# Row sums of a 16384 x 1024 array: each 16-row load made by two transfers, of even and of odd partitions

## The chip, the cores and the metric

The kernel runs on one core of a Trainium2 chip. The metric is the device time of one execution in microseconds (us), taken as the median of several runs. Of the core's engines this kernel uses VectorE (DVE in the profile) and ScalarE (ACT) for the sums, and the queues of SyncE (SP) and ScalarE for issuing transfers between the device's main memory (DRAM) and the on-chip memory of 128 partitions. A transfer's packets are moved by the core's sixteen DMA engines.

## The reference

```python
def setup_inputs():
    batch, seq, dim = 32, 512, 1024
    return {"x": np.random.randn(batch, seq, dim).astype(np.float32)}

def reference(x):
    return np.sum(x, axis=-1).astype(np.float32)
```

So 32 x 512 = 16,384 rows of 1,024 float32 numbers are summed, each to one number: 67.1 MB are read and 65.5 KB written.

## The kernel before

The rows are spread over the 128 partitions, 128 rows to each. They come in two blocks (`BLOCKS = (112, 16)`): in the first, partition p holds rows 112p to 112p + 111 of the array; in the second, 16 consecutive rows of what is left. Inside a partition a block's rows lie one behind another in DRAM, so a transfer of 16 rows takes one contiguous run of 65,536 bytes for each partition.

**The full loads.** The loop `while c < whole` goes over the first block in steps of `G = 16` rows, seven steps. Each step takes one of three buffers `xt` (128 partitions of 16 x 1024 numbers) and fills it by SyncE's queue (line 89): 8,388,608 bytes, all 128 partitions in one transfer. The first step is split: one row of each partition first (512 KB), then the other 15. `rows_dve` (line 47) then lets VectorE sum the 16 rows of all partitions in one TENSOR_REDUCE, into columns of the tile `res`. Only in the seventh step does ScalarE take part: `rows_act` (line 55) sums 7 of the 16 rows, one ACTIVATE each with its sum in an accumulator, which a second instruction reads out. A load into a buffer waits until the reduce that used it three steps earlier has ended, so SyncE's queue stands at such a wait for most of the time, with the two following loads already issued.

**The first block's results.** When the seventh step's sums are done, `res` of the first block (128 x 112 numbers) is stored by two transfers on ScalarE's queue (line 99), one of partitions 0 to 103 and one of 104 to 127. In that queue they stand behind the seven ACTIVATEs and ahead of ScalarE's work on the last 16 rows.

**The tail.** The second block's 16 rows come in five smaller transfers on SyncE's queue: 9, 4 and 2 rows (line 105), and the last row in two pieces of 544 and 480 numbers into a tile of its own, `tail` (line 108). VectorE and ScalarE share the 9 and the 4 rows; of the next two, VectorE sums one by `pairs_dve` (line 67, adding the two halves of a row to each other and summing the pairs), ScalarE the other; VectorE sums the last row in two parts by the same function. At the end a no-op on SyncE's queue waits for ScalarE's last result, and the store of the second block's sums (line 128) waits for VectorE's last.

**What the kernel does to its own program.** After it is built, the first two load instructions of SyncE (`EARLY = 2`) are moved to the program's entry, ahead of the barrier there, so that they start at once; only a load that waits for nothing may be moved. Each transfer signals its end on one of eight semaphores, which are given out in turn; for every load each of the sixteen DMA engines adds one when its share has landed.

Of the kernel before, what the change touches and what calls it, by code (L numbers as in the profile page):

```python
# [1 line left out]

# [4 lines left out]

F32 = mybir.dt.float32
ADD = mybir.AluOpType.add
COPY = mybir.ActivationFunctionType.Copy  # L10
X = mybir.AxisListType.X

BLOCKS = (112, 16)
G = 16
ACT_ROWS = 7
CUT = 544
EARLY = 2


@with_exitstack  # L20
def row_sums(
    ctx: ExitStack,
    tc: tile.TileContext,
    x: bass.AP,
    out: bass.AP,
):
    nc = tc.nc
    P = nc.NUM_PARTITIONS

    x_flat = x.flatten_outer_dims()  # L30
    R, D = x_flat.shape
    C = R // P
    assert R % P == 0 and sum(BLOCKS) == C
    out_flat = out.rearrange("a (b c) -> (a b c)", c=1)

    xpool = ctx.enter_context(tc.tile_pool(name="x", bufs=3))
    rpool = ctx.enter_context(tc.tile_pool(name="res", bufs=1))


    tail = rpool.tile([P, D + 16], F32, name="tail")  # L40
    part = tail[:, CUT + 14 : CUT + 15]
    nc.vector.memset(tail[:, CUT + 15 : CUT + 16], 0.0)  # L42
    seen = rpool.tile([P, 2], F32, name="seen")
    pairs = [rpool.tile([P, D // 2], F32, name=f"pairs{i}") for i in range(3)]

    def rows_dve(xt, res, j, n, c):
        nc.vector.tensor_reduce(  # L47
            out=res[:, c : c + n],
            in_=xt[:, j * D : (j + n) * D].rearrange("p (j d) -> p j d", d=D),
            axis=X,  # L50
            op=ADD,
        )

    def sum_act(v, acc):
        return nc.scalar.activation(out=v, in_=v, func=COPY, accum_out=acc)  # L55

    by_act = []

    def rows_act(xt, res, j, n, c):
        for i in range(n):  # L60
            by_act.append(
                sum_act(xt[:, (j + i) * D : (j + i + 1) * D], res[:, c + i : c + i + 1])
            )

    def pairs_dve(v, a, b, acc, pairs):
        h = (a + b) // 2
        nc.vector.tensor_tensor_reduce(  # L67
            out=pairs[:, 0 : h - a], in0=v[:, a:h], in1=v[:, h:b], scale=1.0, scalar=0.0,
            op0=ADD, op1=ADD, accum_out=acc,
        )  # L70

    def block(r0, n):
        x_b = x_flat[r0 : r0 + P * n].rearrange("(p c) d -> p (c d)", p=P)
        out_b = out_flat[r0 : r0 + P * n].rearrange("(p c) -> p c", p=P)
        return x_b, out_b, rpool.tile([P, n], F32, name=f"res{r0}")

    full = C - G
    done = 0
    for b, n in enumerate(BLOCKS):
        x_b, out_b, res = block(done * P, n)  # L80
        final = b == len(BLOCKS) - 1
        whole = n - G if final else n
        c = 0
        while c < whole:
            m = min(G, whole - c)
            xt = xpool.tile([P, G * D], F32, tag="xt", name="xt")
            parts = (0, 1, m) if done + c == 0 else (0, m)
            for i, k in zip(parts, parts[1:]):
                nc.sync.dma_start(
                    out=xt[:, i * D : k * D], in_=x_b[:, (c + i) * D : (c + k) * D]  # L90
                )
            a = ACT_ROWS if done + c + m == full else 0
            rows_dve(xt, res, 0, m - a, c)
            rows_act(xt, res, m - a, a, c + m - a)
            c += m
        if not final:

            for i, k in ((0, 104), (104, P)):
                nc.scalar.dma_start(out=out_b[i:k], in_=res[i:k])
        done += n  # L100

    xt = xpool.tile([P, G * D], F32, tag="xt", name="xt")
    cuts = [0, 9, 13, 15]
    for i, k in zip(cuts, cuts[1:]):
        nc.sync.dma_start(out=xt[:, i * D : k * D], in_=x_b[:, (c + i) * D : (c + k) * D])  # L105
    last = 15 * D
    for i, k, gap in ((0, CUT, 0), (CUT, D, 16)):
        nc.sync.dma_start(
            out=tail[:, i + gap : k + gap],
            in_=x_b[:, c * D + last + i : c * D + last + k],  # L110
        )

    by_act.clear()
    for i, k in zip(cuts[:2], cuts[1:3]):
        h = (k - i) // 2
        rows_dve(xt, res, i, h, c + i)
        rows_act(xt, res, i + h, k - i - h, c + i + h)
    pairs_dve(xt, 13 * D, 14 * D, res[:, c + 13 : c + 14], pairs[2])
    rows_act(xt, res, 14, 1, c + 14)
    pairs_dve(tail, 0, CUT, part, pairs[0])  # L120


    nc.vector.tensor_copy(out=seen, in_=tail[:, CUT + 14 : CUT + 16])  # L123
    pairs_dve(tail, CUT + 14, D + 16, res[:, c + 15 : c + 16], pairs[1])


    tc.keep_in_program_order(nc.sync.keepalive_nop([nc.sync.lower_ap(res[:, c + 14 : c + 15])]))
    store = nc.sync.dma_start(out=out_b, in_=res)
    for i in by_act:
        tc.declare_no_dep(store.ins, i.ins, reason="the wait is in the nop before it")  # L130


def kernel(tc: tile.TileContext, x: bass.AP, out: bass.AP):
    row_sums(tc, x, out)
    tc.close()
    tc.compile()  # L136

    sp = mybir.EngineType.SP  # L140
    fn = tc.nc.m.functions[0]
    entry, body = None, None
    for blk in fn.blocks:
        ops = [i for i in blk.instructions if i.engine == sp]
        if entry is None:
            entry = blk
        elif any(i.opcode == "DMACopy" for i in ops):
            body = blk
            break
    code = list(body.instructions)  # L150
    loads = [i for i in code if i.engine == sp][:EARLY]
    for load in loads:
        assert load.opcode == "DMACopy" and not load.sync_info.on_wait
        code.remove(load)
    body.instructions = code
    code = list(entry.instructions)
    at = next(k for k, i in enumerate(code) if i.engine == sp and i.opcode == "Drain")
    code[at:at] = loads
    entry.instructions = code

# [1 line left out]
_INS = ['x']  # L162
_OUTS = [((32, 512), 'float32')]


# [23 lines left out]
```

## Time and profile before

| | us |
|---|---|
| median of 7 runs | 161.93 |
| lowest and highest | 161.81, 162.51 |
| the profiled execution | 162.51 |
| its span, first to last instruction | 160.7 |

In the span, by the page:

| engine | busy us | share |
|---|---|---|
| VectorE | 121.5 | 76% |
| ScalarE | 17.2 | 11% |
| GpSimd | 0.2 | 0% |

All x transfers run in one queue of SyncE, the first block's store in ScalarE's. Over the span 418 GB/s are moved on average.

How to read it: the span is cut into 40 slices of 4.02 us, and a row of digits or of GB/s has one entry for each. A packet counts whole in the slice in which it starts, and the large packets here take 2.4 us, so neighbouring slices swing between 294 and 522 GB/s though the transfers go on evenly; the mean over three of them is what counts. A timeline line gives the start, the duration, the engine (with a "q" for its queue), the line in the code, the operation, what it writes and reads, and in brackets the idle time before it and what ended that. A line of transfer issues gives minimum, median and maximum of the issue's own time in ns; the time from issue to landing stands apart. Lines of waits give the total, the number and the longest.

### The profile page before, as it was taken

How to read it: one execution, taken by the hardware profiler on the slowest of the kernel's cores; microseconds unless marked ns; L12 is line 12 of the kernel's file. 1: busy time of each engine (PE TensorE's matmuls, PEld its weight loads, DVE VectorE, ACT ScalarE, POOL GpSimd, SP SyncE). 2: the span in 40 equal slices, each digit the busy share in tenths (PEclk: the TensorE clock that was granted, in tenths of full speed). 3: DMA queues.
4: the chain of work that ended last, by engine and by line, in shares of the span. 5: the costliest groups of instructions: out<-in, count | busy, mean ns of one | idle time of the engine just before them, and what ended most of it. 6: DMA issues, size and time to landing. Idle time of an engine off the chain costs nothing.

```text
span 160.7 us, 122 instructions
## 1 busy us (share of the span) xinstructions
DVE 121.5 (76%) x17; ACT 17.2 (11%) x31; POOL 0.2 (0%) x4
## 2 busy tenths in 40 slices
DVE  0000049998699968999499994999949998598874
ACT  0000000000000000000000000000000000595892
POOL 0000000000000000000000000000000000000000
DMA  9996997997997996996996996996996996999990
GB/s 375 459 474 291 489 506 343 457 506 310 489 489 326 489 489 294 522 489 294 522 489 294 522 489 294 522 489 294 522 489 294 522 489 294 440 431 397 423 387 27
DMA packets 2170, 67.18 MB, mean 418 GB/s; under 512 B 506, under 2 KB 634, under 8 KB 890
## 3 DMA queue, kind: packets, MB, share of 16 engines
q1 hardware_dynamic: 2016, 67.12, 97.1%
q10 hardware_dynamic: 153, 0.06, 0.1%
q14 instruction: 1, 0.00, 0.0%
HBM read 67.11 MB, written 0.07 MB: 418 GB/s over the span
## 4 chain that ended last, share of the span: by engine, by line
DMA 75%; DVE 22%; SPq 0%; issue 0%; DVEq 0%
DMA xt<-in_x_dram 75%; DVE res L47 21%; DVE pairs L67 1%; SPq L105 0%; DVE seen L123 0%; DVE tail L67 0%; DVE res L67 0%; DVEq L136 0%
## 5 line engine op out<-in xcount | busy, mean ns | idle before, releaser
L47 DVE TENSOR_REDUCE res<-xt 128x16 f32<-128x16384 f32 (+3 forms) x9 | 119.8, 13309 | 35.2 <-DMA xt<-in_x_dram 35.2
L55 ACT ACT_TABLE_LOAD x1 | 1.3, 1283 | 138.3 <-DMA xt<-in_x_dram 138.3
L55 ACT ACTIVATE xt<-xt 128x1024 f32<-128x1024 f32 x15 | 15.6, 1044 | 2.4 <-DMA xt<-in_x_dram 2.4
L55 ACT ACTIVATION_READ_ACCUMULATOR xt<-xt 128x1 f32 x15 | 2.8, 187 | 0.0
L42 DVE MEMSET tail<- 128x1 f32 x1 | 0.1, 59 | 1.3 <-PEq L173 1.3
L67 DVE CUSTOM_DVE_ANT_0 pairs<-xt 128x512 f32<-128x512 f32 x1 | 0.7, 692 | 0.4 <-DMA xt<-in_x_dram 0.4
L67 DVE CUSTOM_DVE_ANT_0 pairs<-tail 128x272 f32<-128x272 f32 (+1 forms) x2 | 0.9, 428 | 0.0
L123 DVE COPY seen<-tail 128x2 f32<-128x2 f32 x1 | 0.2, 169 | 0.0
L67 DVE DVE_READ_ACCUMULATOR2_ANT res<- 128x1 f32 x2 | 0.2, 83 | 0.0
L173 POOL MEMSET const-uint8-127<- 128x1 uint8 x1 | 0.1, 102 | 0.0
L173 POOL MEMSET const-bfloat16-1.0<- 128x1 bf16 x1 | 0.1, 101 | 0.0
L173 POOL MEMSET const-float32-0.0<- 128x1 f32 x1 | 0.1, 98 | 0.2 <-issue 0.2
L173 POOL MEMSET const-float32-1.0<- 128x1 f32 x1 | 0.1, 98 | 0.0
L67 DVE DVE_READ_ACCUMULATOR2_ANT tail<- 128x1 f32 x1 | 0.1, 84 | 0.0
## 6 DMA issues: line engine op xcount, KB each, us to landing
xt<-in_x_dram SPq DMA_DIRECT2D x1, 7680.0 KB
xt<-in_x_dram SPq DMA_DIRECT2D x1, 4608.0 KB, 32.4
xt<-in_x_dram SPq DMA_DIRECT2D x1, 2048.0 KB, 36.9
xt<-in_x_dram SPq DMA_DIRECT2D x1, 1024.0 KB, 39.1
xt<-in_x_dram SPq DMA_DIRECT2D x1, 512.0 KB, 4.0
tail<-in_x_dram SPq DMA_DIRECT2D x1, 272.0 KB, 39.2
tail<-in_x_dram SPq DMA_DIRECT2D x1, 240.0 KB, 39.1
xt<-in_x_dram SPq DMA_DIRECT2D x6, 40.8
```

Source lines behind the costliest of these rows:

```text
L42: nc.vector.memset(tail[:, CUT + 15 : CUT + 16], 0.0)
L47: nc.vector.tensor_reduce(out=res[:, c : c + n], in_=xt[:, j * D : (j + n) * D].rearrange("p (j d) -> p j d", d=D), axis=X, op=ADD,)
L55: return nc.scalar.activation(out=v, in_=v, func=COPY, accum_out=acc)
L67: nc.vector.tensor_tensor_reduce(out=pairs[:, 0 : h - a], in0=v[:, a:h], in1=v[:, h:b], scale=1.0, scalar=0.0, op0=ADD, op1=ADD, accum_out ...
L123: nc.vector.tensor_copy(out=seen, in_=tail[:, CUT + 14 : CUT + 16])
L173: nc = _bacc.Bacc("TRN2", target_bir_lowering=False, num_devices=1)
```

## The change

Each of the seven full loads becomes two transfers on SyncE's queue, one of the 64 even partitions and one of the 64 odd ones (`q:P:2`), each of 64 runs of 65,536 bytes. The first step has the same two; its load of one row is gone, so that the two loads moved to the entry are the two halves of the first buffer. The first block's store is written in the program behind the tail's loads instead of ahead of them, and as four transfers, of partitions 0 to 103, 104 to 111, 112 to 119 and 120 to 127, on ScalarE's queue as before.

```diff
@@ -84,19 +84,18 @@
             xt = xpool.tile([P, G * D], F32, tag="xt", name="xt")
-            parts = (0, 1, m) if done + c == 0 else (0, m)
-            for i, k in zip(parts, parts[1:]):
+
+
+            for q in range(2):
                 nc.sync.dma_start(
-                    out=xt[:, i * D : k * D], in_=x_b[:, (c + i) * D : (c + k) * D]
+                    out=xt[q:P:2, 0 : m * D], in_=x_b[q:P:2, c * D : (c + m) * D]
                 )
             a = ACT_ROWS if done + c + m == full else 0
             rows_dve(xt, res, 0, m - a, c)
             rows_act(xt, res, m - a, a, c + m - a)
             c += m
         if not final:
-
-            for i, k in ((0, 104), (104, P)):
-                nc.scalar.dma_start(out=out_b[i:k], in_=res[i:k])
+            out_a, res_a = out_b, res
         done += n
...
@@ -109,6 +108,9 @@
             out=tail[:, i + gap : k + gap],
             in_=x_b[:, c * D + last + i : c * D + last + k],
         )
+
+    for i, k in ((0, 104), (104, 112), (112, 120), (120, P)):
+        nc.scalar.dma_start(out=out_a[i:k], in_=res_a[i:k])
```

## The prediction

> **What bounds the kernel now.** I read the page first: busy shares, the slices, the chain of waits. Then the timeline, to see which engine waits at each stage.
>
> ```profile
> span 160.7 us, 122 instructions
> ...
> DVE 121.5 (76%) x17; ACT 17.2 (11%) x31; POOL 0.2 (0%) x4
> ...
> GB/s 375 459 474 291 489 506 343 457 506 310 489 489 326 489 489 294 522 489 294 522 489 294 522 489 294 522 489 294 522 489 294 522 489 294 440 431 397 423 387 27
> ...
> DMA xt<-in_x_dram 75%; DVE res L47 21%; DVE pairs L67 1%; SPq L105 0%; DVE seen L123 0%; DVE tail L67 0%; DVE res L67 0%; DVEq L136 0%
> ```
>
> VectorE is busy 76% and idle for the rest; the chain is mostly transfers of x. The 21% of VectorE in it looks like a second limit, so the timeline must say who waits for whom.
>
> ```profile
> 22.25 17.22 DVE L47 TENSOR_REDUCE res<-xt 128x16 f32<-128x16384 f32 x1 [20.87 <-DMA xt<-in_x_dram]
> 41.51 17.22 DVE L47 TENSOR_REDUCE res<-xt 128x16 f32<-128x16384 f32 x1 [2.04 <-DMA xt<-in_x_dram]
> 60.87 17.22 DVE L47 TENSOR_REDUCE res<-xt 128x16 f32<-128x16384 f32 x1 [2.14 <-DMA xt<-in_x_dram]
> ...
> 138.27 9.75 DVE L47 TENSOR_REDUCE res<-xt 128x9 f32<-128x9216 f32 x1 [2.13 <-DMA xt<-in_x_dram]
> ...
> 148.11 0.97 ACTq L99 DMA_DIRECT2D out_dram<-res  x2
> ...
> 149.19 1.06 ACT L55 ACTIVATE xt<-xt 128x1024 f32<-128x1024 f32 x1 [2.17 <-DMA xt<-in_x_dram]
> ...
> 156.78 1.06 ACT L55 ACTIVATE xt<-xt 128x1024 f32<-128x1024 f32 x1 [0.21 <-DMA xt<-in_x_dram]
> ...
> 157.74 0.19 ACT L55 ACTIVATION_READ_ACCUMULATOR xt<-xt 128x1 f32 x1
> ...
> 158.37 0.08 DVE L67 DVE_READ_ACCUMULATOR2_ANT res<- 128x1 f32 x1
> 158.49 0.35 SPq L128 DMA_DIRECT2D out_dram<-res  x1
> ```
>
> Each reduce takes 17.22 us and then waits some 2.1 us for the next load. Loads land every (138.27 - 41.51) / 5 = 19.35 us: 8,388,608 bytes in 19.35 us, 433 GB/s. So the rate of the loads is the limit from 22 us to 157 us, VectorE has 2.1 us of slack a load, and only the edges are left: 22.25 - 19.35 = 2.9 us before the first load is flowing, and some 3 us after the last byte.
>
> ```profile
> L89 SPq DMA_DIRECT2D xt<-in_x_dram x8: 327/328/732, 0.0 to 97.5; - x8
> ...
> DMA to landing us min/median/max: 4.0/40.8/59.2
> ...
> L99 ACTq DMA_DIRECT2D out_dram<-res x2: 309/462/615, 148.1 to 148.8; - x2
> ...
> SPq L108 <- DMA xt<-in_x_dram: 0.3, 1, 0.3
> ```
>
> The first two lines are SyncE's issues of the loads: 0.33 us for most, and 40.8 us from issue to landing, so two loads (38.7 us) are already queued ahead of each. The third gives the two stores on ScalarE's queue, 0.31 and 0.62 us. The fourth is a wait of SyncE before a tail transfer, used in a rival below.
>
> The trace's own packet records go one step deeper. The full loads are 768 packets of 65,536 bytes at 2.418 us (most of them alike), eight to each of the sixteen completion increments of a load: 8 x 2.418 = 19.344 us against a period of 19.355. So there is 0.011 us between one transfer and the next, and the engines never run dry.
>
> **The change part by part.** *The loads.* Seven loads were eight transfers and become fourteen. Bytes, the 65,536-byte packets (128 a load) and packets per increment (4 + 4 for 8) stay, if all sixteen engines share a transfer of 64 partitions as they do one of 128. The trace has no transfer of 64 partitions in steps of two, so I bound it. Lower end: the nearest row, the 128-partition load, 19.35 us for 8 MB: nothing added. Upper end: a transfer that names half the partitions runs at half the rate, 38.7 us a load, 7 x 19.35 = 135.5 us added. I take the lower end, since that row has the same packets, queue and bytes; the upper end stays in the range as a rival.
>
> *Six more transfers.* Six more boundaries at 0.011 us are 0.07 us. The tail bounds it from above: its 9 rows come 149.19 - 138.27 = 10.92 us after the load before, 9/16 of 19.355 would be 10.89, so 0.03 us for a boundary; the next one, 154.09 - 149.19 = 4.90 against 4.84, shows 0.06. Six times 0.06 is 0.4. I take 0.07, from the full loads.
>
> *Six more issues on SyncE,* 0.33 us each (up to 0.73, the one at 1.6 us). What is queued behind is the next load's wait for its buffer. They are hidden by the two loads that are in flight; without that cover it would be 0.33 us a load, 2.0 us in all. POOL issues nothing.
>
> *The load of one row goes.* Its 4,096-byte packets took 0.159 us, eight per engine; at the rate of the large ones, 2.418/16 = 0.151. That is 8 x 0.008 = 0.07 us gained. Two of the sixteen increments are late from there on: of the row's, fourteen are in by 3.42 us and the last at 4.03; of the first full load 21.55 and 22.15; of the last tail transfer 157.40 and 158.02. Everything waits for the slowest, so 0.6 us would be won if the small packets cause this, and nothing if starting does. I take 0.15, nearer to nothing, because one 61,440-byte packet of the second transfer (3.10 us where others took 2.27) is part of that lag. VectorE gets nothing earlier from the halves: its reduce reads all partitions.
>
> *The stores.* They stay behind the seven activations on ScalarE's queue, and the loads they now follow in the text are on SyncE's, so the move shifts no work. Four for two: the pair ends at 149.08; two more at 0.31 to 0.62 end at 149.70 to 150.31. Behind them on ScalarE are the rows that start at 149.19, so these are 0.51 to 1.12 us late. The gap of 0.21 us before 156.78 absorbs part; ScalarE ends at 157.93 + 0.30 to 0.91 = 158.23 to 158.84. SyncE's last store waits for ScalarE and for VectorE's 158.45: 0 to 0.4 us. I take 0, by the shorter issue, as the later store was.
>
> Sum: 0 + 0.07 - 0.07 - 0.15 + 0 = -0.15 us. The profiled execution took 162.51 us (160.7 of span, 1.8 around it), the highest of the seven; the median, 161.93, is 0.58 lower. So 162.51 - 0.15 - 0.58 = 161.8 us. Its own range, with the bounds: -0.67 to +0.8 on 161.93, 161.2 to 162.7.
>
> [...] The row says 433 GB/s in 128-partition transfers, 65,536 / 2.418 = 27.1 GB/s an engine. [...]
>
> **The rivals.** *The half transfers run at half the rate (the other side).* Place: the seven full loads. For: the loads are the bound with no slack, and all engines run at one steady rate in step (fourteen of sixteen increments within 0.5 us), so two that got in each other's way would do so in every packet rather than drift apart. Against: packets, bytes and queue are those of the nearest row. Price: 135.5 us, 161.9 + 135.5 = 297 us. It decides early: 2% off the rate costs 2.7 us, more than every edge term together. An in-between case, half of the packets disturbed, gives some 161.9 + 68 = 230 us.
>
> *A wait in the tail takes over.* The loads use eight completion semaphores in turn, and SyncE's wait before the last tail transfer (0.3 us, the fourth line above) is for the load that last used its one. With fourteen load transfers the turn comes sooner; if a tail transfer had to wait for the last full load (138.27 us), the queue would be empty then and the start-up of a transfer would show: 4.0 us from issue to landing for the one-row load, less the 1.2 us of its bytes, 2.8 us. Against: by count, the last two of the tail's five come back to halves of the fifth and the sixth full load, and the sixth has landed by 118.9 us. Time: 161.9 + 2.8 = 164.7.
>
> *The start gains all of it:* the lag of two engines goes with the small packets: 161.9 - 0.67 = 161.2, inside the forecast's own range.
>
> **How the numbers follow.** This kernel's measurement can tell 0.2%, 0.3 us, from no change. The forecast's case, no loss of rate, has 0.44: 0.22 faster (below 161.6; the start gives more than I took), 0.19 the same, 0.03 slower. Half rate has 0.41, the in-between case 0.06, the tail's wait 0.09; all three are slower. Sums: faster 0.22, same 0.19, slower 0.59. The likeliest single case is the first, so 161.8 us is the predicted time, with its own range of 161.2 to 162.7; but it and the tail's wait hold little over half, so the range must reach the half rate's 297, plus the edge bounds and a few more boundaries: 161.2 to 300.
>
> **What would show it.** The distance from one 16-row reduce's start to the next: 19.35 to 19.5 us means the rate held, 38.7 us the half rate, and VectorE's idle time before them would go from 2.1 to 21 us. The packets of 65,536 bytes: 2.42 us or near 4.8. First reduce at or before 22.25 us; its start tells the edge term. Four stores on ScalarE's queue from 148.11 and the activation behind them at about 149.7; the last store's issue still at 158.5. A gap in the transfers after 138 us would be the tail's wait. The prediction is wrong if the full loads come at another pace than 19.35 us, or if the last store is held by ScalarE by more than 0.4 us.

## The result, and the profile after

The changed kernel takes 162.60 us (median of 16 runs, 162.47 to 162.74), the kernel before 161.97 us in the same sessions. The ratio is 1.0034, with a 95% interval of 1.0026 to 1.0042: slower by about 0.55 us, a third of a percent (0.42 to 0.68 by the interval; the plain medians differ by 0.63). The profiled execution took 162.81 us, 161.0 of it span, and is slower than all sixteen.

The first lines of the changed kernel's page, and its chain of waits by line:

```profile
span 161.0 us, 137 instructions
...
DVE 121.5 (75%) x17; ACT 17.1 (11%) x31; POOL 0.2 (0%) x4
...
DMA xt<-in_x_dram 63%; DVE res L47 27%; ACT xt L55 5%; ACTq L113 1%; SPq L90 1%; ACTq L138 0%; DVEq L47 0%; ACTq L55 0%
```

The work is the same, and transfers still carry the chain. New in it are ScalarE's activations (5%) and the two issuing queues: SyncE's line 90, the issue of the loads, and ScalarE's line 113, that of the stores. The timeline shows where they stand:

```profile
22.51 17.22 DVE L47 TENSOR_REDUCE res<-xt 128x16 f32<-128x16384 f32 x1 [20.55 <-DMA xt<-in_x_dram]
41.87 17.22 DVE L47 TENSOR_REDUCE res<-xt 128x16 f32<-128x16384 f32 x1 [2.15 <-DMA xt<-in_x_dram]
...
138.60 9.76 DVE L47 TENSOR_REDUCE res<-xt 128x9 f32<-128x9216 f32 x1 [2.12 <-DMA xt<-in_x_dram]
...
148.45 1.65 ACTq L113 DMA_DIRECT2D out_dram<-res  x4
...
150.19 1.06 ACT L55 ACTIVATE xt<-xt 128x1024 f32<-128x1024 f32 x1 [2.75 <-DMA out_dram<-res]
...
158.42 0.08 DVE L67 DVE_READ_ACCUMULATOR2_ANT res<- 128x1 f32 x1
158.43 0.19 ACT L55 ACTIVATION_READ_ACCUMULATOR xt<-xt 128x1 f32 x1
158.78 0.35 SPq L130 DMA_DIRECT2D out_dram<-res  x1
```

The rate held: (138.60 - 41.87) / 5 = 19.35 us a load, as before. In the packet records the 65,536-byte packets still have a median of 2.418 us. What moved are the two ends. The first reduce starts at 22.51 us, and four stores hold ScalarE's queue from 148.45 to 150.10, so that ScalarE ends after VectorE (158.62 against 158.50) and the last store waits for it. The question is which end the 0.55 us are lost at, or whether a part goes in between.

### The profile page after: what moved, and what is told of

It reads as the page before. It is cut to its first block, busy times and chain, and to the rows that moved or that the text cites. A ratio compares the mean times of both kernels' runs of the same rounds, so it can differ in the third digit from the quotient of the medians.

```text
span 161.0 us, 137 instructions
## 1 busy us (share of the span) xinstructions
DVE 121.5 (75%) x17; ACT 17.1 (11%) x31; POOL 0.2 (0%) x4
## 4 chain that ended last, share of the span: by engine, by line
DMA 63%; DVE 27%; ACT 5%; ACTq 1%; SPq 1%; issue 0%; DVEq 0%
DMA xt<-in_x_dram 63%; DVE res L47 27%; ACT xt L55 5%; ACTq L113 1%; SPq L90 1%; ACTq L138 0%; DVEq L47 0%; ACTq L55 0%
```

## The experiments

All medians are set against the kernel before, run on the same chip in the same session (161.96 us in the first four runs, 162.11 in the next four, 162.16 in three, 162.20 in the last).

### Undoing one part at a time

Two stores for four, the first buffer as before, and both:

```diff
 after_two_stores
-    for i, k in ((0, 104), (104, 112), (112, 120), (120, P)):
+    for i, k in ((0, 104), (104, P)):
 after_row_first
-            for q in range(2):
+            if done + c == 0:
+                for i, k in ((0, 1), (1, m)):
+                    nc.sync.dma_start(
+                        out=xt[:, i * D : k * D], in_=x_b[:, (c + i) * D : (c + k) * D]
+                    )
+            else:
+              for q in range(2):
...
 after_row_first_two: both edits
```

> The changed kernel with the first block's store in two transfers again. Theory 1 (two causes: the first load starts later, and four stores hold ScalarE): the activation behind the stores starts at about 149.5 us instead of 150.19, ScalarE ends before VectorE, the last store is issued at 158.5 instead of 158.78, and the time falls by 0.25 us to about 162.35. Rival A (the stream of even and odd transfers loses it all): 162.6, unchanged. Rival B (it is all lost at the start): 162.6, unchanged.

> The changed kernel with the first buffer loaded as before, one row and then 15 of all partitions; the other six loads stay even and odd, and the four stores stay. Theory 1: the first reduce starts at about 22.2 us instead of 22.51; VectorE's path ends 0.3 us earlier, ScalarE's too, and the time is 162.2 to 162.3. Rival A: 162.6. Rival B: 162.0, as before the change.

> Both undone: the first buffer as before and two stores; only six loads are even and odd. Theory 1 and rival B: 162.0 us, the time before the change, within 0.1. Rival A: 162.5 or more, as six of seven loads keep the split.

Measured: 162.58 us (ratio 1.0037, 1.0024 to 1.0050) with two stores: nothing gained. 162.10 us (1.0008, 1.0000 to 1.0017) with the first buffer as before, four stores kept: most of the loss is gone. 162.18 us (1.0013, 1.0004 to 1.0021) with both. So rival B was nearest: the loss is at the start. Theory 1 fell in its second half, though its mechanism is in the profile. The activation behind two stores starts at 149.30 us, not 150.19, and ScalarE then ends at 157.86, well before VectorE; but from the first reduce to the end of the span it is 138.53 us in that profile and 138.51 in the changed kernel's, and the median doesn't move. In these two profiles ScalarE's hold delays the last store by only 0.11 us, counted from the first reduce (136.27 against 136.16): VectorE itself ended 0.14 us sooner in the changed kernel's execution. One execution each can't say more.

### The stores alone

```diff
 before_four_stores
-            for i, k in ((0, 104), (104, P)):
+            for i, k in ((0, 104), (104, 112), (112, 120), (120, P)):
                 nc.scalar.dma_start(out=out_b[i:k], in_=res[i:k])
```

> The kernel before with four stores for two, nothing else. Theory 1: two more issues, 0.6 us, on ScalarE behind which its last rows stand; by the profile before it ends at 157.93 + 0.67 - 0.21 = 158.39 us, against VectorE's 158.45, so the price is hidden there or shows by 0.1 to 0.2 us: 162.0 to 162.15. A rival in which the stores cost 0.3 us in any case: 162.3.

Measured: 162.16 us, ratio 1.0014 (1.0002 to 1.0026), 0.03 to 0.4 us. The timeline of this kernel:

```profile
147.71 1.66 ACTq L99 DMA_DIRECT2D out_dram<-res  x4
...
149.48 1.06 ACT L55 ACTIVATE xt<-xt 128x1024 f32<-128x1024 f32 x1 [2.86 <-DMA out_dram<-res]
...
157.71 0.19 ACT L55 ACTIVATION_READ_ACCUMULATOR xt<-xt 128x1 f32 x1
157.75 0.08 DVE L67 DVE_READ_ACCUMULATOR2_ANT res<- 128x1 f32 x1
158.06 0.35 SPq L128 DMA_DIRECT2D out_dram<-res  x1
```

Four issues take 1.66 us where two took 0.97, and ScalarE and VectorE now end together; the last store leaves 0.2 us after VectorE's end. Without ScalarE in the way it left within 0.04 us of it (158.49 after 158.45 in the first profile). So the bound of the prediction, 0 to 0.4, held, the value of 0 was a little low for the kernel before, and in the changed kernel the runs can't tell the stores' price from nothing.

### The first load: its first packet, its packets' size, or the split itself

```diff
 before_no_row
-            parts = (0, 1, m) if done + c == 0 else (0, m)
+            parts = (0, m)
 before_first_evenodd: the first of the seven loads by q:P:2, the other six whole (in place of the loop over parts)
+            if done + c == 0:
+                for q in range(2):
+                    nc.sync.dma_start(
+                        out=xt[q:P:2, 0 : m * D], in_=x_b[q:P:2, c * D : (c + m) * D]
+                    )
+            else:
+                nc.sync.dma_start(out=xt[:, 0 : m * D], in_=x_b[:, c * D : (c + m) * D])
 before_row_then_evenodd: the same, with a whole first row ahead
+                nc.sync.dma_start(out=xt[:, 0:D], in_=x_b[:, 0:D])
+                for q in range(2):
+                    nc.sync.dma_start(out=xt[q:P:2, D : m * D], in_=x_b[q:P:2, D : m * D])
```

> The kernel before without its load of one row: the first buffer comes in one transfer of all 128 partitions, packets of 65,536 bytes from the start. Theory S (the step of two partitions makes the first transfer slow to start: its issue takes 0.54 us for 0.37, the first packet comes at 1.33 us for 1.00): the first packet stays at 1.0 us, the first reduce starts at 21.7, 162.0 us. Theory P (a first transfer of large packets starts up slower): the first reduce starts at 22.1, 162.4 us.

> The kernel before with the first of its seven loads alone made by even and odd partitions (no load of one row, two stores). Both S and P: first reduce at 22.2 to 22.5 us and 162.5, the whole loss. Rival A (the other six even and odd loads cost as well): 162.4 or less.

> The kernel before with its load of one row as it is (all partitions, the first transfer) and the other 15 rows of the first buffer by even and odd partitions. If the loss is in starting the very first transfer (its issue and its first packet), nothing is lost: first packet at 1.0 us, first reduce at 21.6 to 21.9, within 0.1 us of the kernel before. If even and odd transfers cost wherever they stand in the first load, 0.3 us more than before.

Measured: 162.22 us (1.0006, 0.9997 to 1.0015) without the row; 162.47 us (1.0020, 1.0011 to 1.0028) with the first load split; 162.18 us (1.0000, 0.9991 to 1.0009) with a whole row first and the rest of that load split. The start of these three on SyncE's queue and VectorE, first without the row:

```profile
0.00 0.38 SPq L89 DMA_DIRECT2D xt<-in_x_dram  x1
...
21.90 17.22 DVE L47 TENSOR_REDUCE res<-xt 128x16 f32<-128x16384 f32 x1 [20.51 <-DMA xt<-in_x_dram]
```

then with the first load by even and odd partitions:

```profile
0.00 0.55 SPq L89 DMA_DIRECT2D xt<-in_x_dram  x1
...
22.27 17.22 DVE L47 TENSOR_REDUCE res<-xt 128x16 f32<-128x16384 f32 x1 [20.30 <-DMA xt<-in_x_dram]
```

and with a whole row ahead of the split:

```profile
0.00 0.38 SPq L88 DMA_DIRECT2D xt<-in_x_dram  x1
...
21.83 17.22 DVE L47 TENSOR_REDUCE res<-xt 128x16 f32<-128x16384 f32 x1 [20.10 <-DMA xt<-in_x_dram]
```

The issue of the first transfer took 0.55 us where it was split and 0.37 to 0.38 where it was whole. By the packet records the first packet then starts at 1.33 us instead of 1.00. Nothing is in flight at that moment, and the first reduce starts at 22.27 us for 21.90 without the row and without a split. The longer issue is 0.18 of the 0.33 us; where the other 0.15 arise isn't shown. Put a whole row ahead, and split transfers behind it cost nothing that the runs can tell (1.0000): they are issued from 0.43 to 2.07 us, before the row has landed, 3.6 us after its own issue. So theory S holds in that the split makes the very first transfer slow to start, and theory P is worth 0.1 us by the median and at most 0.24 by the interval. It isn't the step of two partitions, as theory S had it: the kernel by halves below, without a step, has the same 0.55 us and a first packet at 1.32 us. Its transfers share with these the 64 partitions.

### The kernel before again, and a sum for all of them

> The kernel before once more, for a profile of a run near its median: in the nine profiles so far with a steady stream the time from the first reduce's start to the span's end is 138.5 us, so a run of about 162.0 us should start its first reduce at 160.2 - 138.5 = 21.7 us, not at the 22.25 of the profile the prediction was made from. If instead the first reduce starts at 22.2 again and the end comes sooner, the loss isn't all in the first load.

Measured: 162.14 us, ratio 1.0001 (0.9993 to 1.0010), which shows what these comparisons can resolve. Its profiled execution, 162.10 us, has:

```profile
0.00 0.37 SPq L89 DMA_DIRECT2D xt<-in_x_dram  x1
...
21.97 17.22 DVE L47 TENSOR_REDUCE res<-xt 128x16 f32<-128x16384 f32 x1 [20.59 <-DMA xt<-in_x_dram]
```

Not 21.7, as expected, but earlier than the 22.25 of the first profile. In that first one two of the load's sixteen increments came 0.5 to 0.6 us behind the rest; here all of them lie within 0.52 us (21.35 to 21.87). One packet of 3.10 us for 2.27 there belonged to that execution, not to the kernel. Now the span of each profile can be cut at the first reduce's start:

| kernel | first packet | first reduce | from there to the end | median of its runs | ratio |
|---|---|---|---|---|---|
| before, first profile | 1.00 | 22.25 | 138.48 | 161.97 | |
| before, again | 1.00 | 21.97 | 138.34 | 162.14 | 1.0001 |
| before_four_stores | 0.99 | 21.84 | 138.55 | 162.16 | 1.0014 |
| before_row_then_evenodd | 1.00 | 21.83 | 138.56 | 162.18 | 1.0000 |
| before_no_row | 1.01 | 21.90 | 138.53 | 162.22 | 1.0006 |
| after_row_first | 1.00 | 21.64 | 138.53 | 162.10 | 1.0008 |
| after_row_first_two | 1.01 | 21.77 | 138.56 | 162.18 | 1.0013 |
| before_first_evenodd | 1.33 | 22.27 | 138.46 | 162.47 | 1.0020 |
| after_two_stores | 1.32 | 22.16 | 138.53 | 162.58 | 1.0037 |
| after | 1.33 | 22.51 | 138.51 | 162.60 | 1.0034 |

The third column spreads over 0.9 us, the fourth over 0.2, and there the changed kernel lies in the middle. All kernels whose first transfer is whole start the first reduce by 21.97 us, but for the one odd profile; the three with a split first transfer at 22.16 or later. So in these profiles what one execution loses against another is lost before its first load has landed. Each row is a single execution, though, the first 0.54 us above the median of its kernel and the last 0.21, so the third column shows differences between executions as well as between kernels; the ratios are what compares kernels. What isn't located is a rest: with a whole first row, six split loads still show 1.0008 and 1.0013, 0.13 and 0.21 us. Six more boundaries of 0.011 us would be 0.07 us, 0.0004, which is inside the first interval and at the edge of the second. In the profiles the time from the first to the seventh load's landing is 116.10 us in the kernel before, in its repeat and after the change, 116.11 in both kernels with a whole first row, and 116.13 with two stores: the stream itself can hold at most 0.03 us of it.

### Which partitions: even and odd, or halves

The prediction's great rival was the half rate. The split that the change doesn't use tests whether a transfer of half the partitions can run that slowly at all:

```diff
 after_halves
             for q in range(2):
+                s = slice(q * P // 2, (q + 1) * P // 2)
                 nc.sync.dma_start(
-                    out=xt[q:P:2, 0 : m * D], in_=x_b[q:P:2, c * D : (c + m) * D]
+                    out=xt[s, 0 : m * D], in_=x_b[s, c * D : (c + m) * D]
                 )
```

> The changed kernel with partitions 0 to 63 and 64 to 127 in place of even and odd. If the rate goes with the stretch of partitions that a transfer reaches, each half runs at half the rate: packets near 4.8 us, reduces 38.7 us apart, 297 us. If it goes with the sixteen engines alone, it is as with even and odd: packets of 2.42 us, 162.6 us.

Measured: 310.35 us, ratio 1.91. Its timeline, and three windows (columns: the stretch, its length, busy time of VectorE, ScalarE and GpSimd, the clock of TensorE, the busy share of the DMA engines, GB/s):

```profile
43.83 17.22 DVE L47 TENSOR_REDUCE res<-xt 128x16 f32<-128x16384 f32 x1 [41.86 <-DMA xt<-in_x_dram]
84.28 17.22 DVE L47 TENSOR_REDUCE res<-xt 128x16 f32<-128x16384 f32 x1 [23.23 <-DMA xt<-in_x_dram]
124.70 17.22 DVE L47 TENSOR_REDUCE res<-xt 128x16 f32<-128x16384 f32 x1 [23.20 <-DMA xt<-in_x_dram]
```

```profile
30.00:70.00 40.00, 17.22 (x1) 0.00 (x0) 0.00 (x0) 1.00 1.01 210
70.00:110.00 40.00, 17.22 (x1) 0.00 (x0) 0.00 (x0) 1.00 1.01 210
110.00:150.00 40.00, 17.22 (x1) 0.00 (x0) 0.00 (x0) 1.00 1.01 210
```

The DMA engines are busy throughout (a share of 1.01, and each load's transfer still gets sixteen increments), yet a 65,536-byte packet takes 5.06 us in the mean for 2.42, and a load 40.4 us: 7 x (40.4 - 19.35) = 147 us added, 310 in all. What keeps the engines busy at half the bytes no run shows. The edit changes which partitions a transfer writes and, with them, which rows of x it reads from DRAM at a time; no run separates the two. The list that each engine got isn't in the records, so why even and odd partitions kept 433 GB/s where halves ran at 210 isn't shown.

### What a short split transfer ahead does

Three kernels put the load of one row into even and odd partitions, to separate the slow issue from the large packets. They showed something else.

```diff
 before_row_evenodd (EARLY = 3), before_row_evenodd_2 (EARLY = 2)
+                for q in range(2):
+                    nc.sync.dma_start(out=xt[q:P:2, 0:D], in_=x_b[q:P:2, 0:D])
+                nc.sync.dma_start(out=xt[:, D : m * D], in_=x_b[:, D : m * D])
 row_and_rest_evenodd (EARLY = 2): the 15 rows split too
+                for i, k in ((0, 1), (1, m)):
+                    for q in range(2):
+                        nc.sync.dma_start(
+                            out=xt[q:P:2, i * D : k * D], in_=x_b[q:P:2, i * D : k * D]
+                        )
```

> The kernel before with its load of one row made by two transfers, even and odd partitions; the other 15 rows and all later loads take whole transfers, and three loads are moved to the entry for two. Theory S: first packet at 1.33 us, first reduce 0.3 to 0.5 us later than with a whole first row, 162.3 to 162.5. Theory P: the packets are small, so no loss, 162.0 to 162.1.

> As before_row_evenodd (the load of one row by even and odd partitions), but with two loads moved to the entry for three. If the slow start of a transfer in steps of two partitions is the whole loss: 0.3 to 0.4 us more than before. If that run's 2.7 us came from this shape and not from the third load ahead of the barrier, about 2.7 us more again.

> As before_row_evenodd_2, with the other 15 rows of the first buffer by even and odd partitions too. If that run's 2.7 us came from the step from two short split transfers to one whole transfer, it goes: first packet at 1.33 us, some 0.3 to 0.5 us more than before, 162.5. If it came from the short transfers being over before the next one's packets are there, it stays: 164.9.

Measured: 164.85 us (1.0165, 1.0151 to 1.0179), 164.93 us (1.0171, 1.0157 to 1.0185) and 163.73 us (1.0097, 1.0080 to 1.0114). Neither theory had this size, and the third kernel lies between its two expectations, 162.5 and 164.9. That a third load was moved ahead of the barrier isn't the cause, since the second kernel does without. In the second one's timeline

```profile
0.00 0.55 SPq L89 DMA_DIRECT2D xt<-in_x_dram  x1
...
25.02 17.22 DVE L47 TENSOR_REDUCE res<-xt 128x16 f32<-128x16384 f32 x1 [23.05 <-DMA xt<-in_x_dram]
```

the first reduce is 3 us late, and again all the loss lies ahead of it (138.25 us from there on). By the packet records the row has landed by 3.7 us; the 61,440-byte packets of the other rows start between 3.0 and 5.4 us (2.5 to 3.7 us in the kernel before) and the first of them take up to 3.3 us for 2.27; the load's last increment comes 2.3 us after the median one. With the rest split as well it is 0.6 us. This fits engines that have run out of the short transfer's packets before the next one's are there, but no run shows it. Why some of these packets start as late as 5.4 us, with the issue over at 2.2, stays open.

## Why the prediction was wrong

The forecast was 161.8 us, no loss of rate, and the direction was wrong: the changed kernel is slower, at the upper end of that case's own range (161.2 to 162.7). Its case was right, its sum was not. That 162.60 lies in that range is luck: the room above was 0.4 us for boundaries and 0.4 for the stores, and the loss is in neither; slower without a loss of rate had a chance of 0.03. Step by step:

- **The loads' rate: right.** Nothing was added to the full loads, 19.35 us each. The choice of the nearest row, the 128-partition load, held; half the rate was a real risk, as the kernel by halves shows, but one that these partitions didn't meet. That naming half the partitions halves the rate, the 38.7 us a load behind the 297 us, was an assumption of mine that no trace of before shows, as is the chance of 0.41 put on it; measured were 19.35 us a load by even and odd partitions and 40.4 by halves. The reason given for the choice, "the same packets, queue and bytes", is as true of the halves, which ran at 210 GB/s, so it doesn't decide between the two, and that it gave the right answer here is luck.
- **Six more issues on SyncE, "hidden by the two loads that are in flight": this step failed, at the first load.** The six that were added are hidden: from the first landing to the seventh the stream is longer by at most 0.03 us. What the step left out is that the first load's own issues become those of 64-partition transfers, and there no load is in flight. The sum had nothing for this, and put a gain on the start instead. Measured: the first transfer's issue is 0.55 us for 0.37 and its first packet comes 0.33 us later; the first load alone split, its row gone with it, costs 0.32 us (1.0020; 0.18 to 0.45), and a whole row ahead of the split takes that away (1.0000). The issue rows of the trace were all of 128-partition transfers, and I took their 0.33 us for 64 partitions too; after the change an issue takes 0.47 to 0.61:

```profile
L90 SPq DMA_DIRECT2D xt<-in_x_dram x14: 472/584/612, 0.0 to 98.3; - x14
```

- **The load of one row goes, -0.07 and -0.15: wrong sign.** Without it, and without a split, the kernel shows 1.0006 (0.9997 to 1.0015): 0.1 us lost by the median, at best 0.05 won. I also misread the row's increments: fifteen of its sixteen were in by 3.42 us and one was late, at 4.03, where I had two. The lag of two engines that I hoped to win back belonged to the one execution I had; it was the slowest of seven, by 0.34 us over the next, and the repeat's profile doesn't have it. I had even subtracted 0.58 us for that execution, and then counted part of the same excess as a gain.
- **Six boundaries, +0.07: a little high.** In the profiles the stream is longer by 0.03 us at most.
- **The stores, 0 of a bound of 0 to 0.4: in the bound.** ScalarE's activation started at 150.19 us, inside the foretold 149.70 to 150.31, and ScalarE did end after VectorE, by 0.12 us; yet taking two stores away gave nothing.
- **The tail's wait: it came, at no price, and my count of it was wrong.** Because the four stores took their places in the turn of semaphores between the tail's transfers, three of these waited for the sixth and the seventh load and the last one for the tail's own 9 rows; the landings on each semaphore show that order (119.17, 128.83 and 138.51 us, then 149.44). SyncE's waits and the last tail issue of the changed kernel:

```profile
SPq L107 <- DMA xt<-in_x_dram: 19.9, 2, 10.6
```

```profile
149.45 0.33 SPq L107 DMA_DIRECT2D tail<-in_x_dram  x1
```

It was issued at 149.45 us instead of 118.91, and landed at 158.06, 8.6 us later, behind what was still queued. The cover of some 8 us is what is left of 39; what a store or two more in that turn would cost, no run shows.

With the measured terms the sum would have been 0.32 us for the split first load (0.1 of it shows with the row gone and no split), at most 0.03 for the stream and nothing for the stores, as two fewer changed nothing: some 0.35 us, against 0.55 measured (0.42 to 0.68 by the interval). The other 0.2 us aren't located. They are of the size of the 0.13 and 0.21 us that six split loads show behind a whole first row, whose intervals reach from 0 to 0.34.

No kernel tried beats the one before; the nearest, a whole first row with split rows behind it, equals it.

## What to carry to other kernels

"Hidden by what is in flight" has to be asked of each instance of a moved or added instruction, the first one above all: with two loads in flight the split issues lengthened the stream by at most 0.03 us in all, and at 0.0 us one put the first packet back by 0.33 us. Before a lag in a profile is counted as a gain, see that it is in more than one execution, above all if the profiled one is the slowest of its group. And if a transfer must be split by partitions, try even and odd ones before halves: here even and odd kept 433 GB/s, halves fell to 210.

## What the runs showed of the hardware

- The issue of a 64-partition transfer took 0.47 to 0.64 us on SyncE's queue, with a step of two partitions or without, though it has half the packets of a 128-partition one, which took 0.33 to 0.48 (but for one at 1.6 us in the kernel before, 0.70 to 0.73, and one at 1.2 us in before_row_evenodd, 0.58).
- Large packets at the very start were slower than later: the first 65,536-byte packets took 2.4 to 3.5 us for 2.42, in whole and in even and odd transfers alike (2.76 to 3.44 for the first sixteen of the changed kernel), and the next sixteen 2.42 to 2.44. Starting with a row of 4,096-byte packets instead saved at most 0.15% of the time.
- Two short split transfers ahead of a large one cost 1.0 to 1.7%, far more than the 0.33 us of the first packet.
